# Own weight buffers for the projections, frames normed ahead, and an earlier place for tile 1 and the short tile

## The chip, the cores and the metric

The kernel runs on one core of a Trainium2 chip. The metric is the device time of one execution in microseconds (us). The engines named below are PE (matrix multiply), DVE (vector), ACT (scalar), POOL (which issues the indirect DMAs) and SP (which issues the other DMAs). Each engine takes its instructions in the order in which the program has them.

## The reference

One layer of a streaming encoder, for 1024 new frames (8 tiles of 128 frames, called 0 to 7) and for 32 frames of a running stream (the short tile, called S):

```python
h = rms_norm(x, norm_mix_w)
proj = h @ w_in                                   # 1024 -> 3608 columns
o1 = gla(...)                                     # gated linear attention, a recurrence over chunks
o2 = gated_delta_net(conv(...))                   # gated delta rule, a recurrence over chunks
x = x + concat(o1, o2) @ w_out
# PEER: 8 heads, product keys; 16 experts of 16384 for each head and frame
q = rms_norm(x, norm_ffn_w) @ peer_wq
eidx, gate = top_16_of_product_keys(q, k1, k2)    # 128 experts for each frame
act = gelu(einsum('thkd,td->thk', peer_u[eidx], xblk))
x = x + einsum('thk,thkd->td', gate * act, peer_v[eidx])
y = rms_norm(x, norm_final_w)
```

## The kernel before

The work falls into three parts that overlap in time.

**The mixers and the routing.** The input projections are made in four groups, PROJ = [0, S], [1, 2, 3], [4, 5, 6], [7], by the generator `project(g)`. It loads its tiles of x, norms and transposes them (three frames of 128 in a group of three, "its frames"; PE writes `ptr`), and then multiplies with chunks of `w_in` of 256 KB that `chunk` loads: 17 units by channel (PE writes `pcm`) and 6 by token (PE writes `ptm`). Groups 1 and 2 split weights and frames into a rounded part and a rest (`wh`, `wl`, `hh`, `hl`); groups 0 and 3 multiply float32 directly. For each tile, in the order 0, S, 1, 2, ... 7, come then the mixers: `gdn_free`, `gla`, and `gdn_state` (the part of the delta rule that needs the state of the tile before). When a group of tiles is through, `out_proj` (PE writes `pwo`) and `route` (PE writes `pq` and `psc`) follow, and `select`, a chain of small DVE operations that picks the 128 experts of each frame. At the end of `select` the row numbers `ef`/`ei` of the experts are made, and `prepare_rows` transposes them on PE (`pe`). Tile 0 is its own routing group; its rows come in two halves.

**The dense tiles.** For tiles 2 to 5 all 16384 experts are computed with matmuls (`dense`: PE writes `pD` and `pV`, in three passes each). Before that, `gate_matrix` lays their gates out.

**The gathered tiles.** For tiles 0, S, 1, 6 and 7 the rows of `peer_u` and `peer_v` are fetched with indirect DMAs that POOL issues, each of 128 rows of 1024 floats (512 KB). `u_phase(t)` fetches 128 such tiles `ug` (32 for S) and DVE multiplies each with the frames and sums it into a column of `act` (line 1063); after the last one, `act` goes through a gelu and PE transposes it (`pw`). `v_phase(t)` fetches 128 tiles `vg` (32 for S) in rounds of four, and PE adds each round up in eight matmuls (`pv`, line 1108). A u-tile of tile 0 or S uses the three buffers of the pool `ge`; in later tiles every fourth one uses a buffer of the pool `gp`, which is opened once the projections' pool `p1` is closed. `act` has two buffers.

What stands where on an engine is decided by a scheduler when the program is built. It starts from the order in which the generators are woven together (`weave` takes one step of each in turn); steps under `urgent` have a high priority. GATHERS gives the order of the gathered tiles.

## Time and profile before

| | |
|---|---|
| time, median of 3 runs | 3464.75 us (3453.7 to 3467.83) |
| the profiled execution | 3470.48 us, of which its span 3468.8 us |
| busy in the span | PE 90%, DVE 66%, POOL 38%, ACT 37% |
| DMA | 974.88 MB, mean 281 GB/s |
| chain that ended last | PE 66%, DVE 14%, DMA 10%, issue 5% |

The span can be cut at places that the trace shows: the last matmul of the first projection at 117 us, the first gather at 249 us, the last gather for tile 0 at 601 us, the first dense matmul at 1737 us, the last dense matmul at 3342 us. A busy PE is not a PE at its peak, since its matmuls are pipelined; float32 matmuls have two records each in the trace, the rounded ones (`pD`, `pV`, and the `pcm` and `ptm` of groups 1 and 2) have one.

### The profile page before, as it was taken

How to read it: one execution, taken by the hardware profiler on the slowest of the kernel's cores; microseconds unless marked ns; L12 is line 12 of the kernel's file. 1: busy time of each engine (PE TensorE's matmuls, PEld its weight loads, DVE VectorE, ACT ScalarE, POOL GpSimd, SP SyncE). 2: the span in 40 equal slices, each digit the busy share in tenths (PEclk: the TensorE clock that was granted, in tenths of full speed). 3: DMA queues.
4: the chain of work that ended last, by engine and by line, in shares of the span. 5: the costliest groups of instructions: out<-in, count | busy, mean ns of one | idle time of the engine just before them, and what ended most of it. 6: DMA issues, size and time to landing. Idle time of an engine off the chain costs nothing.

```text
span 3468.8 us, 50260 instructions
## 1 busy us (share of the span) xinstructions
PE 3113.4 (90%) x17730; PEld 2469.2 (71%) x17730; DVE 2305.9 (66%) x6165; ACT 1298.7 (37%) x2703; POOL 1312.4 (38%) x1168
## 2 busy tenths in 40 slices
PE   8873778999999888989589999999999999999974
PEld 6662677998898767877367777777777777777630
DVE  3557878664388998999867677766766765434420
ACT  5322445665323226899523232222222322212210
POOL 3004443000001354353545555555555553233454
PEclk9986878999999899989699999999999999999986
DMA  6368888445745789999999998989998997767898
GB/s 197 88 210 261 277 282 272 129 133 153 234 129 175 250 321 350 330 343 329 319 345 357 338 345 335 349 334 349 356 335 325 366 345 283 253 240 278 288 341 297
DMA packets 373455, 974.88 MB, mean 281 GB/s; under 512 B 37345, under 2 KB 139186, under 8 KB 369106
## 3 DMA queue, kind: packets, MB, share of 16 engines
q0 software_dynamic: 156672, 570.49, 45.8%
q1 hardware_dynamic: 216386, 400.64, 34.1%
q8 instruction: 140, 2.29, 0.3%
q14 instruction: 113, 0.93, 0.1%
q10 hardware_dynamic: 144, 0.52, 0.0%
HBM read 908.73 MB, written 62.76 MB: 280 GB/s over the span
## 4 chain that ended last, share of the span: by engine, by line
PE 66%; DVE 14%; DMA 10%; issue 5%; ACT 4%; POOL 1%; another core or an unknown queue 0%; SPq 0%; POOLq 0%; ACTq 0%; DVEq 0%
PE pV L186 6%; PE pD L187 6%; PE pV L188 6%; PE pV L187 6%; PE pD L186 6%; PE pD L188 6%; PE pv L1108 6%; PE pq L537 3%; DVE ug L1063 3%; PE pwo L501 3%; DMA ug<-u,ei 3%; DMA vg<-v,eiT 2%; PE ptm L440 2%; PE ptm L430 2%; PE pcm L332 1%
## 5 line engine op out<-in xcount | busy, mean ns | idle before, releaser
L1062 POOL DMA_INDIRECT ug<-u,ei x512 | 624.9, 1221 | 1111.5 <-DVE ug L1063 467.4
L1102 POOL DMA_INDIRECT vg<-v,eiT x488 | 567.5, 1163 | 895.9 <-PE pv L1108 450.3
L1063 DVE SCALAR_TENSOR_TENSOR ug<-ug,h 128x1024 f32<-128x1024 f32 x544 | 658.7, 1218 | 129.8 <-DMA ug<-u,ei 118.7
L187 PE MATMUL pD<-hh,ul 128*128 128x512 f32 x1024 | 402.2, 393 | 10.9 <-DVE ul L181 10.9
L186 PE MATMUL pD<-hh,uh 128*128 128x512 f32 x1024 | 402.0, 393 | 1.6 <-ACT uh L180 1.6
L188 PE MATMUL pD<-hl,uh 128*128 128x512 f32 x1024 | 401.8, 392 | 0.0
L187 PE MATMUL pV<-vh,wl 128*128 128x512 f32 x1024 | 398.7, 391 | 0.0
L188 PE MATMUL pV<-vl,wh 128*128 128x512 f32 x1024 | 398.2, 391 | 0.0
L186 PE MATMUL pV<-vh,wh 128*128 128x512 f32 x1024 | 378.4, 393 | 0.0
L1108 PE MATMUL pv<-vg,wd 128*32 128x512 f32 x1952 | 293.4, 661 | 57.7 <-DMA vg<-v,eiT 57.7
L180 ACT CAST vh<-vx 128x1024 fp32r<-128x1024 f32 x128 | 129.2, 1050 | 556.1 <-PE pV L187 471.7
L1003 DVE TENSOR_TENSOR acc<-acc,pV 128x512 f32<-128x512 f32 x256 | 168.8, 684 | 246.2 <-PE pV L188 228.0
L537 PE MATMUL pq<-h2T,wqb 128*128 128x256 f32 (+2 forms) x1280 | 257.8, 356 | 9.3 <-DMA wqb<-wq 6.4
L977 ACT ACTIVATE w<-pD 128x512 f32<-128x512 f32 x128 | 76.6, 598 | 504.3 <-PE pD L188 476.8
L537 PEld LDWEIGHTS pq<-h2T,wqb 128*128 128x128 f32 x1280 | 216.5, 198 | 35.1 <-DMA wqb<-wq 6.6
L187 PEld LDWEIGHTS pD<-hh,ul 128*128 128x128 f32 x1024 | 192.7, 188 | 66.0 <-issue 12.6
L186 PEld LDWEIGHTS pV<-vh,wh 128*128 128x128 f32 x1024 | 191.8, 188 | 58.8 <-issue 12.6
L186 PEld LDWEIGHTS pD<-hh,uh 128*128 128x128 f32 x1024 | 192.7, 188 | 54.5 <-issue 10.1
L188 PEld LDWEIGHTS pD<-hl,uh 128*128 128x128 f32 x1024 | 192.7, 188 | 52.5 <-issue 12.6
L188 PEld LDWEIGHTS pV<-vl,wh 128*128 128x128 f32 x1024 | 192.2, 188 | 51.0 <-issue 10.9
L187 PEld LDWEIGHTS pV<-vh,wl 128*128 128x128 f32 x1024 | 192.2, 188 | 47.1 <-issue 7.5
L180 ACT CAST wh<-w 128x512 fp32r<-128x512 f32 x244 | 149.9, 617 | 143.9 <-DVE w L983 53.3
(333 smaller groups left out, 5606.6 us busy)
## 6 DMA issues: line engine op xcount, KB each, us to landing
vx<-v SPq DMA_DIRECT2D x128, 512.0 KB
ux<-ut SPq DMA_DIRECT2D x127, 512.0 KB
wqb<-wq SPq DMA_DIRECT2D x80, 576.0 KB
gd<-gst SPq DMA_DIRECT2D x16, 2048.0 KB
G<-gd SPq DMA_DIRECT2D x32, 1024.0 KB
w<-win_c SPq DMA_DIRECT2D x96, 256.0 KB
wch<-wout SPq DMA_DIRECT2D x40, 512.0 KB
w<-win_t SPq DMA_DIRECT2D x72, 256.0 KB
```

The costliest lines, as they stand in the source:

```text
L180: nc.scalar.copy(hi, x)
L186: mm(out, a[0], b[0], start=first, stop=False, **kw)
L187: mm(out, a[1], b[0], start=False, stop=False, **kw)
L188: mm(out, a[0], b[1], start=False, stop=last, **kw)
L501: mm(p[:n, :P], mixT[t][:, kb, :], w[:, kb, :], start=(kb == 0), stop=(kb == KB - 1))
L537: mm(p[:, :N], w[:, kb, :], h2T[:, kb, :], start=(kb == 0), stop=(kb == KB - 1))
L977: nc.scalar.activation(w, pD, AF.Gelu_apprx_tanh)
L1003: nc.vector.tensor_tensor(acc[ti][:, cs], acc[ti][:, cs], p, op=ALU.add)
L1062: nc.gpsimd.indirect_dma_start(out=g, out_offset=None, in_=A["u"], in_offset=idx_of(ei[:, k:k + 1]))
L1063: nc.vector.scalar_tensor_tensor(g, g, 1.0, h2, op0=ALU.mult, op1=ALU.mult, accum_out=act[:, k:k + 1])
L1102: nc.gpsimd.indirect_dma_start(out=g, out_offset=None, in_=A["v"], in_offset=idx_of(eiT[:, tok:tok + 1]))
L1108: return mm(pv[half][c * 32:(c + 1) * 32, :], wd[:, c, :], vs[c][:, half * 512:(half + 1) * 512], start=(r == 0), stop=(r == ns - 1), tile ...
```

## The change

`project` takes its weight chunks from buffers of its own (`w`, two of them, in the pool `p1`), and no longer from the four `wqb` buffers that it shared with the routing; `wqb` has three. Group 0 turns through four kinds of buffers. Group 3, which had turned through `wqb`, `wh` and `wl`, eight buffers in all, has the two. The transposed frames of group 0 lie in the buffer `h2T`, and no longer in `hh`, which is group 1's from the start.

The frames of a group are normed and transposed ahead of its weights: `frames_of(1)` stands before tile 0, `frames_of(2)` behind tile S, `frames_of(3)` behind tile 2. Group 2 is woven with tile 2, group 3 with tile 3 (before: group 2 with tiles 1 and 2, group 3 with tile 2).

Tile 1 is treated as tile 0 was: its `gdn_state` follows at once, then the routing of the group [1, S] and the selection of both. The gathers begin with `peer_u` of 0, S and 1, all of them urgent, and `peer_v` of 0 follows.

```diff
-COMING = {1: [(1, None)], 2: [(2, 24)], 3: [(2, None), (3, None)]}
-
-BGN = [0, 0, 0, 0, 24, 14, 14, 14, 14, 14]
+COMING = {1: [1], 3: [2], 4: [3]}
+
+AT_ONCE = [0, 1]
+
+BGN = [0, 0, 0, 0, 14, 14, 14, 14, 14, 14]
...
+WQ = 3
...
-GATHERS = [([0, "S"], []), ([1], [0]), ([6], ["S", 1]), ([7], [6]), ([], [7])]
+GATHERS = [([0, "S", 1], []), ([], [0]), ([6], ["S", 1]), ([7], [6]), ([], [7])]
...
         if direct:
-            hx = p1.tile([P, KB, N], F32, name="hx", tag="hh")
+            hx = rt.tile([P, KB, N], F32, name="hx", tag="h2T") if first else p1.tile([P, KB, N], F32, name="hx", tag="hh")
...
             loads[0] += 1
-            own = direct and (None, "wh", None, "wl")[loads[0] % 4]
-            if own:
-                w = p1.tile(list(src.shape), F32, name="w" + own, tag=own, bufs=WB)
+            own = ("w", "wqb", "wh", "wl")[loads[0] % 4] if first else "w"
+            if own == "wqb":
+                w = rt.tile(list(src.shape), F32, name="w", tag="wqb", bufs=WQ)
             else:
-                w = rt.tile(list(src.shape), F32, name="w", tag="wqb", bufs=4)
+                w = p1.tile(list(src.shape), F32, name="w", tag=own, bufs=WB)
...
-            w = rt.tile([P, KB, P], F32, name="wch", tag="wqb", bufs=4)
+            w = rt.tile([P, KB, P], F32, name="wch", tag="wqb", bufs=WQ)
...
-            w = rt.tile([P, KB + 1, P], F32, name="wqb", tag="wqb", bufs=4)
+            w = rt.tile([P, KB + 1, P], F32, name="wqb", tag="wqb", bufs=WQ)
...
-            e = t in (0, "S") or k % 4 < 3
+            e = t in EARLY or k % 4 < 3
...
+    def frames_of(g):
+
+        weave(some(projects[g], len(PROJ[g])))
+
+    frames_of(1)
+    last = None
     for k in range(len(ORDER) + 1):
-        cur, prev = (ORDER[k] if k < len(ORDER) else None), (ORDER[k - 1] if k > 1 else None)
-        parts = [selecting(), some(behind, BGN[k])]
-        parts.append(chain(*(some(projects[g], n) for g, n in COMING.get(k, []))))
-        if prev is not None:
-            parts.append(gdn_state(prev))
+        cur = ORDER[k] if k < len(ORDER) else None
+        parts = [selecting(), some(behind, BGN[k]), chain(*(projects[g] for g in COMING.get(k, [])))]
+        if last is not None:
+            parts.append(gdn_state(last))
         if cur is not None:
             parts += inputs(cur)
         weave(*parts)
-        if k == 0:
-
+        if k in COMING and COMING[k][-1] + 1 in projects:
+            frames_of(COMING[k][-1] + 1)
+        ready_now = finished(last) if last is not None else []
+        last = cur
+        if cur in AT_ONCE:
             weave(gdn_state(cur))
-            finished(cur)
-            weave(routing(GROUPS[0]))
-            weave(selecting())
+            last = None
+            for g in finished(cur):
+                weave(routing(g))
+                weave(selecting())
...
-        us = [urgent(u_phase(t, *sel[t])) if t in (0, "S") else u_phase(t, *sel[t]) for t in us]
+        us = [urgent(u_phase(t, *sel[t])) if t in EARLY else u_phase(t, *sel[t]) for t in us]
```

What the scheduler makes of it shows in the order of the instructions, here at three places. The first is PE at the end of the routing of tile 0: `pq` and `psc` are the routing's matmuls, `pe` the transpose of the chosen row numbers `ef`, `ptr` a transpose of frames, `pcm` a unit of the projection of group 1. Before:

```order
L537 MATMUL pq<-h2T,wqb 128x128 x8
L543 MATMUL psc<-wqb,qb 128x128
L1035 MATMUL pe<-ident,ef 128x128
L313 MATMUL ptr<-ident,x 128x128 x24
L332 MATMUL pcm<-hh,wh 128x384 x4
L332 MATMUL pcm<-hl,wh 128x384 x4
```

And in the changed kernel:

```order
L540 MATMUL pq<-h2T,wqb 128x128 x8
L546 MATMUL psc<-wqb,qb 128x128
L1038 MATMUL pe<-ident,ef 128x128
L217 MATMUL psm<-ident,row 128x64 x3
L237 MATMUL pdg<-aA_132,tri 128x12
L374 MATMUL pn<-ones,sq 128x1 x3
L335 MATMUL pcm<-hh,wh 128x384 x4
```

The 24 transposes of frames are gone from here, and so are 264 of the 408 `pcm` matmuls of group 1: they stand ahead of these rows, among the mixers and the routing of tile 0. `pe` still stands right behind the last `psc`.

The second place is POOL's queue from the first gather on: `ug<-u,ei` is a gather of `peer_u` for tile 0 in the first row and for tile 1 in the later rows, `ug<-u,eiS` one for S, `vg<-v,eiT` one of `peer_v` for tile 0. Before:

```order
L1062 DMA ug<-u,ei 128x1024 x128
L1102 DMA vg<-v,eiT 128x1024 x5
L1062 DMA ug<-u,ei 128x1024
L1062 DMA ug<-u,eiS 128x1024 x32
L1062 DMA ug<-u,ei 128x1024 x6
L1102 DMA vg<-v,eiT 128x1024 x4
L1062 DMA ug<-u,ei 128x1024 x4
```

And in the changed kernel:

```order
L1065 DMA ug<-u,ei 128x1024 x128
L1065 DMA ug<-u,eiS 128x1024 x32
L1065 DMA ug<-u,ei 128x1024 x10
L1105 DMA vg<-v,eiT 128x1024 x4
L1105 DMA ug<-v,eiT 128x1024
L1105 DMA vg<-v,eiT 128x1024
L1065 DMA ug<-u,ei 128x1024 x118
```

Before, the gathers of `peer_u` for tile 1 and of `peer_v` for tile 0 take turns by fours; now 118 gathers for tile 1 stand in one piece, and nearly all of `peer_v` of tile 0 stands behind them.

The third place is the end of PE's program, at the last dense matmul (`pV`); `pv_28316` and `pv_28317` are the two halves of the sums of `peer_v` for tile 7. Before:

```order
L187 MATMUL pV<-vh,wl 128x512
L188 MATMUL pV<-vl,wh 128x512
L1108 MATMUL pv_28316<-vg,wd 32x512
L1108 MATMUL pv_28316<-ug,wd 32x512 x2
L1108 MATMUL pv_28316<-vg,wd 32x512
L1108 MATMUL pv_28317<-ug,wd 32x512 x2
```

And in the changed kernel:

```order
L190 MATMUL pV<-vh,wl 128x512
L191 MATMUL pV<-vl,wh 128x512
L1111 MATMUL pv_28316<-vg,wd 32x512 x4
L1111 MATMUL pv_28317<-vg,wd 32x512 x4
L1111 MATMUL pv_28316<-ug,wd 32x512 x4
L1111 MATMUL pv_28317<-ug,wd 32x512 x4
```

From the last `pV` to the end of the program there stand 152 `pv` matmuls before, which are 19 rounds of four gathers, and 56 in the changed kernel, which are 7 rounds.

## Rows read from the trace of the kernel before

**Rows 1.** The page: busy time by engine, and the chain that ended last.
```profile
PE 3113.4 (90%) x17730; PEld 2469.2 (71%) x17730; DVE 2305.9 (66%) x6165; ACT 1298.7 (37%) x2703; POOL 1312.4 (38%) x1168
PE 66%; DVE 14%; DMA 10%; issue 5%; ACT 4%; POOL 1%; another core or an unknown queue 0%; SPq 0%; POOLq 0%; ACTq 0%; DVEq 0%
```

**Rows 2.** Stretches: us, busy and (records) of PE, PEld, DVE, ACT, POOL; clock, DMA.
```profile
117.00:249.00 132.00, 110.85 (x913) 94.16 (x911) 78.42 (x397) 34.90 (x120) 0.00 (x0) 0.92 0.40 124
249.00:304.00 55.00, 5.24 (x39) 4.65 (x39) 43.03 (x154) 9.66 (x31) 23.74 (x25) 0.59 0.79 249
304.00:602.00 298.00, 222.64 (x1303) 205.36 (x1303) 237.07 (x521) 139.36 (x264) 124.69 (x104) 0.82 0.85 279
602.00:1093.00 491.00, 478.11 (x3534) 444.85 (x3534) 318.15 (x1277) 240.50 (x557) 5.63 (x6) 0.97 0.52 159
1093.00:1737.00 644.00, 541.55 (x3495) 448.93 (x3493) 593.32 (x2226) 382.37 (x1021) 282.05 (x232) 0.89 0.91 312
1737.00:3342.00 1605.00, 1591.79 (x7619) 1186.12 (x7619) 993.94 (x1449) 426.55 (x562) 778.07 (x655) 1.00 0.88 324
3342.00:3462.00 120.00, 62.28 (x306) 12.20 (x304) 7.84 (x20) 1.65 (x4) 65.66 (x69) 0.67 0.91 327
```

**Rows 3.** Waits in 304 to 601 us: us in total, times, longest.
```profile
PE pe L1035 <- DVE ef L1026: 48.9, 1, 48.9
DVE ug L1063 <- DMA ug<-u,ei: 37.3, 28, 3.4
```

**Rows 4.** Timeline of POOL: tile 0's first, fourth, one slow and last gather.
```profile
249.28 1.13 POOL L1062 DMA_INDIRECT ug<-u,ei  x1 [211.23 <-DVE vt L552]
...
255.32 1.34 POOL L1062 DMA_INDIRECT ug<-u,ei  x1 [2.42 <-DVE vt L549]
...
366.26 3.86 POOL L1062 DMA_INDIRECT ug<-u,ei  x1 [0.30 <-issue]
...
600.59 0.94 POOL L1062 DMA_INDIRECT ug<-u,ei  x1 [2.00 <-DVE ug L1063]
```

**Rows 5.** Groups on DVE and POOL, 249 to 602 us, and POOL after 3342.
```profile
L1063 DVE SCALAR_TENSOR_TENSOR ug<-ug,h 128x1024 f32<-128x1024 f32 x125 | 152.3, 1220 | 49.9 <-DMA ug<-u,ei 48.7 <-issue 0.6 <-DVE XT L741 0.2
L1062 POOL DMA_INDIRECT ug<-u,ei x128 | 148.4, 1160 | 415.1 <-DVE vt L552 213.2 <-DVE ug L1063 129.8 <-DVE hist L392 9.7
L1102 POOL DMA_INDIRECT vg<-v,eiT x37 | 35.2, 953 | 24.8 <-PE pv L1108 16.2 <-issue 8.5
```

**Rows 6.** Timeline of POOL: the first, fourth and last gather for S.
```profile
1111.07 0.94 POOL L1062 DMA_INDIRECT ug<-u,eiS  x1 [24.04 <-DMA eiS<-ei]
...
1118.10 0.94 POOL L1062 DMA_INDIRECT ug<-u,eiS  x1 [3.61 <-DVE ug L1063]
...
1197.29 0.94 POOL L1062 DMA_INDIRECT ug<-u,eiS  x1 [0.99 <-DVE sc L551]
```

**Rows 7.** Timeline of PE: a round in the dense stage and its neighbours.
```profile
3303.36 0.39 PE L187 MATMUL pD<-hh,ul 128*128 128x512 f32 x1
3303.59 0.39 PE L188 MATMUL pD<-hl,uh 128*128 128x512 f32 x1
3303.91 1.92 PE L1108 MATMUL pv<-vg,wd 128*32 128x512 f32 x16
3305.76 0.50 PE L186 MATMUL pD<-hh,uh 128*128 128x512 f32 x1
```

**Rows 8.** Timeline of PE: tile 7's first round, the last pV, rounds behind it.
```profile
3253.94 1.06 PE L1108 MATMUL pv<-vg,wd 128*32 128x512 f32 x8
...
3341.92 0.39 PE L188 MATMUL pV<-vl,wh 128*128 128x512 f32 x1
3343.12 0.62 PE L1108 MATMUL pv<-vg,wd 128*32 128x512 f32 x1 [0.81 <-DMA vg<-v,eiT]
...
3362.34 3.40 PE L1108 MATMUL pv<-vg,wd 128*32 128x512 f32 x16 [3.35 <-DMA vg<-v,eiT]
3367.83 2.76 PE L1108 MATMUL pv<-ug,wd 128*32 128x512 f32 x16 [2.09 <-DMA ug<-v,eiT]
...
3457.96 1.03 PE L1108 MATMUL pv<-vg,wd 128*32 128x512 f32 x1 [6.61 <-DMA vg<-v,eiT]
```

**Rows 9.** The chain in order of time: start us, us, what.
```profile
57.58 4.13 DMA wwl<-win_t
...
370.42 7.24 DMA ug<-u,ei
...
574.85 5.60 DMA w<-win_s
...
600.95 1.90 PE ptr L313 x8
...
606.61 5.88 PE pcm L332 x32
...
1154.10 8.42 DMA ug<-u,eiS
```

**Rows 10.** Waits of PE in 1093 to 1737 us.
```profile
PE pq L537 <- DMA wqb<-wq: 6.4, 1, 6.4
```

**Rows 11.** A group on ACT, 250 to 602 us.
```profile
L95 ACT ACT_TABLE_LOAD x10 | 12.8, 1283 | 0.2
```

More of the change, by code (lines that the diff above doesn't have):

```diff
@@ L275, in project @@
             if t == tiles[0]:
-                nmix = rt.tile([P, D], F32, name="nmix", tag="wqb", bufs=4)
+                nmix = rt.tile([P, D], F32, name="nmix", tag="wqb", bufs=WQ)
                 nc.sync.dma_start(nmix, bass.AP(tensor=A["nmix"].tensor, offset=A["nmix"].offset, ap=[[0, P], [1, D]]))
@@ L516, in route @@
         h2T = rt.tile([P, KB, N], F32, name="h2T", bufs=1)
-        nffn = rt.tile([P, D], F32, name="nffn", tag="wqb", bufs=4)
+        nffn = rt.tile([P, D], F32, name="nffn", tag="wqb", bufs=WQ)
         nc.sync.dma_start(nffn, bass.AP(tensor=A["nffn"].tensor, offset=A["nffn"].offset, ap=[[0, P], [1, D]]))
@@ L1229, in layer_kernel @@
             gp = ctx.enter_context(tc.tile_pool(name="gp", bufs=1, side="right", reuse_waits="tile"))
-        for g in finished(prev) if prev is not None else []:
+        for g in ready_now:
             behind = chain(behind, routing(g))
```

## The prediction

> **What bounds the kernel now.** The page first: PE is busy in 90% of the span and holds 66% of the chain that ended last, DVE 14%, DMA 10% [rows 1]. Such shares mix stages, so the stretches come next [rows 2], and they show five regimes. From 117 to 249 us PE works on tile 0's mixers and routing, with 21 of 132 us idle. From 249 to 304 us it does next to nothing (5.2 us): the waits name it, 48.9 us of PE standing at `pe` for the row numbers `ef` [rows 3]. From there to 602 us, while `peer_u` of tile 0 is gathered, PE is idle for a quarter, and DVE is busy for 237 of 298 us. From 602 to 1093 us POOL is all but idle (5.6 us) and PE is the bound (478 of 491 us). From 1093 to 1737 us DVE is (593 of 644). The dense stage is PE's alone (1592 of 1605, clock 1.00). Behind the last `pV` comes a tail of 120 us in which PE waits for gathers, at a clock of 0.67.
>
> **The change, step by step.** The sum is made against the profiled execution: 3470.5 us, its span and 1.7 us around it, 5.7 us over the median of the runs.
>
> *The tail.* 19 rounds follow the last `pV`, now 7. The first starts at 3343.12 and the nineteenth at 3457.96 [rows 8]: 18 steps, 6.4 us each. 12 rounds fewer: -77 us.
>
> *The dense stage.* The order puts 102 rounds between the first `pD` and the last `pV`, where 92 were. A round stretches the step between two dense matmuls from 0.23 us to 2.17 us [rows 7], so it costs PE 1.9 to 2.0 us: +20 us. Can the gathers keep up? The order spaces tile 7's 25 rounds there by 31 to 32 matmuls, 24 dense ones and one round, some 7.4 us. Before, 13 rounds of tile 7 went from 3253.94 to the one just ahead of the last `pV` [rows 8], 7 us apart, with PE busy throughout. I take no wait.
>
> *Tile 0 up to its first gather (249.28 us, [rows 4]).* 24 transposes and 264 `pcm` matmuls now lie ahead of it on PE. 32 `pcm` take 5.88 us, 8 transposes 1.90 [rows 9]: 264 x 0.184 + 24 x 0.24 = 54 us. 21 fit into PE's idle time, if that can be used at all: +33 (bounds 0 and +54). The 48.9 us at `pe` stay, because nothing was put between the last `psc` and it; the filling work went ahead of the wait and lengthens the way to it.
>
> *`peer_u` of tile 0.* 127 steps from 249.28 to 600.59 [rows 4], 2.77 us each, over three buffers; the order puts 540 DVE instructions beside them, where 529 were, so I keep the 352 us. What is gained is that PE stands at its 2,354th matmul at the end, and not at its 1,880th.
>
> *From there to PE's 4,147th matmul*, where the projections are about done in the changed kernel; before it stood there at 1093 us. PE's rate in 602 to 1093 us is 2,267 matmuls in 491 us. Now 1,793 are left: 388 us. Two things are new in this stretch. The selections of tiles 1 and S end in a `pe` again: up to the first of them there are 445 matmuls, 97 us, but 499 DVE instructions, at 0.25 us (318 us for 1,277 records) 125 us: +28 (bounds 0 and +49, a wait like tile 0's). And S's 32 gathers stand packed, with 228 matmuls (49 us) beside them. Before, S took 86 us for 31 steps; its first buffer came round in 7.0 us [rows 6], which over three buffers is 2.3 us a gather. 32 of these and one landing come to about 87: +38 (bounds 0 and +50). Sum 388 + 28 + 38 = 454 against 491, which with the 33 from above leaves PE 4 us ahead.
>
> *From the 4,147th matmul to the dense stage.* Tile 1's gathers can't go on before: `act` has two buffers, tile 1 takes tile 0's, and the transpose `pw` that frees it stands there, because its PSUM bank is the projections' until then. The DVE work up to the dense stage is the same (1,644 instructions, 1,653 before). But 118 gathers of tile 1 now stand in one piece, on three buffers, 5 to 6 DVE instructions apart (tile 0's: 4). That is near tile 0's case: 2.77 us a gather, 327 us, with DVE busy 79% (280 of 353 us; 48.7 us go at the landings of `ug` [rows 2, 5]) instead of the 92% of 1093 to 1737 us. 327 x (1 - 0.79/0.92) = +46 (bounds 0, if the landings are covered as they were, and +99, at 3.2 us a gather).
>
> Edits taken as nothing: `wqb` with three buffers for four (`pq` waited 6.4 us for it in 644 [rows 10]; twice that would be +6); 22 more table loads on ACT at 1.28 us [rows 11], 28 us, hidden on an engine that is busy for 382 of 644 us, and 28 if each came where others wait; group 0's nine buffers for eight; the frames normed ahead.
>
> Sum: +33 - 37 + 46 = +42 for the start of the dense stage, +20 in it, -77 behind it: -15. On the profiled execution that is 3455, on the median 3450 us.
>
> **A rule weighed.** POOL needs 1160 ns to issue a gather while DVE is 79% busy and 953 ns when DVE is nearly idle [rows 2, 5]; one took 3.86 us, and the next waited for nothing but that [rows 4]. The Trainium skill ("SBUF — State Buffer", section "SBUF: two separate sides") says that the descriptors of POOL's DMAs are written through a port that certain DVE operations hold for their whole length, so that such a DMA looks blocked by DVE. By that rule the piece of 118 gathers beside a busy DVE would be the wrong place for them; its example, some 3,100 ns in place of 620, would make 118 x (3.1 - 2.77) = +39 us. The trace shows 0.2 us of it, which POOL's 415 us of idle time in that stretch swallow.
>
> **The rivals.** *Tile 1 starves DVE* (the slower side). A buffer comes round in a landing and a product: 7.24 + 1.22 us over three buffers is tile 0's pace, 8.42 + 1.22, a landing of S's, makes 3.2 us a gather [rows 5, 9]: 118 x 0.45 = +53 on the forecast, 3503 us. For it: the routing's weights and the gate matrices run beside it. Against it: the DMA engines' share was 0.84 to 0.85 in tile 0's stretch too, and the pace there was 2.77. It decides from 3.05 us a gather on (33 us over the forecast).
>
> *The waits are hidden.* If S's packed gathers, the selection and tile 1's piece cost no more than their DVE work, 28 + 38 + 46 = 112 us fall away: 3338 us; with half of it, which is more likely, 3394. For it: in 304 to 601 us DVE waited for only 28 landings, 3.4 us at most [rows 3]. Against it: tile 0's pace, with the same buffers.
>
> *Group 3 lacks buffers.* It had eight weight buffers and has two, for 58 chunks, with 630 matmuls of PE's order about them, 137 us, 2.4 us a chunk. A chunk takes 4.1 to 5.6 us to land [rows 9] and about 0.9 in use; over two buffers that is 2.5 to 3.3 us: +6 to +52, up to 3502. SP takes its DMAs in order, so a chunk that waits for its buffer holds up the routing's weights behind it.
>
> *The tail only moves.* If the 12 rounds that went into the dense stage wait there as they did behind it (2 to 3.8 us of PE's idle time each [rows 8]), +36: 3486 us. The 13 of before speak against it.
>
> *POOL is held up by DVE*, as the 3.86 us of [rows 4] was: 118 x 1.09 = +129, 3579 us. It was the exception among 128.
>
> **How the numbers follow.** The sum as it stands, give or take 20 us, has 45 in 100; the hidden waits 22, tile 1 starved 17, group 3 eight, the tail five, POOL three. A measurement of this kernel tells about 0.5% (17 us) from no change. So below 3447 us there are the second case and nearly half of the first: 0.42. Above 3482 lie tile 1, group 3, POOL and a part of the tail's case: 0.29, and 0.29 in between. The range reaches to the half-hidden case and past the starved one, 3385 to 3515 us; the first case alone has 3430 to 3470.
>
> **What would show it.** Behind the last `pV` some 45 us with 7 rounds; a dense stage of 1625 us that starts at about 1780 us; tile 0's first gather at 280 us and a wait of PE at `pe` of about 50 us right behind it; tile 1's 118 gathers in one piece of 310 to 340 us. I would be wrong if the dense stage starts before 1740 us (the waits were hidden) or after 1815 (tile 1 or group 3), or if PE shows idle time at `pv` before the last `pV`.

## The result, and the profile after

The changed kernel takes 3510.7 us (median of 4 runs, 3504.6 to 3513.2), the kernel before beside it 3466.3 us: a ratio of 1.0129, with a 95% interval of 1.0096 to 1.0162. The forecast was 3450 us; the time lies inside the range, on its slower side.

The page first: busy time by engine and the chain that ended last, as [rows 1].

```profile
PE 3130.6 (89%) x17730; PEld 2497.2 (71%) x17730; DVE 2316.9 (66%) x6165; ACT 1327.2 (38%) x2725; POOL 1282.3 (37%) x1168
...
PE 61%; DVE 13%; DMA 11%; issue 11%; ACT 3%; POOL 1%; SPq 0%; POOLq 0%; another core or an unknown queue 0%; ACTq 0%; DVEq 0%
```

PE has the same 17,730 records and 17 us more busy time, in a span that is 38 us longer (3507.1, before 3468.8). A page like this can't say where they went. The stretches of the changed kernel can (columns as in [rows 2]); their bounds are the legs of the prediction: the first gather, the end of `peer_u` of tile 0, PE's 4,147th matmul, its 5,000th, the first `pD`, the last `pV`. A matmul's number is its place in the program's order, looked up in the trace; two kernels with different orders can have different matmuls under one number.

```profile
117.00:301.00 184.00, 168.77 (x1251) 149.37 (x1251) 116.35 (x509) 78.68 (x191) 0.00 (x0) 0.95 0.46 142
301.00:353.00 52.00, 9.29 (x59) 8.01 (x57) 37.65 (x151) 12.24 (x36) 24.52 (x21) 0.60 0.75 238
353.00:679.00 326.00, 257.39 (x1628) 236.95 (x1629) 245.39 (x534) 127.70 (x259) 129.65 (x107) 0.85 0.82 273
679.00:906.00 227.00, 181.25 (x1127) 163.50 (x1127) 195.70 (x846) 96.39 (x238) 35.24 (x34) 0.83 0.48 156
906.00:1148.00 242.00, 225.36 (x1735) 210.88 (x1734) 122.59 (x404) 131.39 (x267) 3.17 (x3) 0.97 0.58 175
1148.00:1496.00 348.00, 275.60 (x1640) 245.07 (x1639) 324.81 (x1111) 139.79 (x388) 129.73 (x120) 0.85 0.84 277
1496.00:1839.00 343.00, 278.97 (x1871) 215.86 (x1869) 266.28 (x1083) 246.21 (x630) 133.13 (x123) 0.90 0.93 321
1839.00:3453.00 1614.00, 1612.03 (x7778) 1189.54 (x7778) 965.58 (x1398) 424.72 (x557) 772.55 (x663) 1.00 0.88 325
3453.00:3507.00 54.00, 20.48 (x114) 4.20 (x112) 5.81 (x9) 3.29 (x8) 21.25 (x22) 0.74 0.75 271
```

The dense stage is PE's alone as before (1612 of 1614 us), and 54 us follow the last `pV` where 127 did. What is lost lies ahead: the dense stage starts at 1839 us and not at 1737. The row to remember is 1148 to 1496 us: DVE is busy for 93% of it and PE for 79%. Three more views fill this in. First the timeline of POOL (start, length, what ended the idle time): tile 0's first and last gather, S's first, the first of tile 1, the first behind the wait for `act`, the first and the last of the 118 in one piece.

```profile
301.21 1.13 POOL L1065 DMA_INDIRECT ug<-u,ei  x1 [261.26 <-DVE ei L1030]
...
678.58 1.08 POOL L1065 DMA_INDIRECT ug<-u,ei  x1 [2.35 <-DVE ug L1066]
...
827.64 0.94 POOL L1065 DMA_INDIRECT ug<-u,eiS  x1 [147.98 <-DVE row L403]
...
905.73 1.15 POOL L1065 DMA_INDIRECT ug<-u,ei  x1 [1.75 <-DVE ug L1066]
...
1150.14 1.68 POOL L1065 DMA_INDIRECT ug<-u,ei  x1 [237.89 <-DVE ug L1066]
...
1175.75 0.94 POOL L1065 DMA_INDIRECT ug<-u,ei  x1 [0.30 <-DVE it L556]
...
1533.76 1.15 POOL L1065 DMA_INDIRECT ug<-u,ei  x1 [1.53 <-DVE ug L1066]
```

Then the waits from 301 to 679 us, which answer to [rows 3]:

```profile
PE pe L1038 <- DVE ef L1029: 39.6, 1, 39.6
...
DVE ug L1066 <- DMA ug<-u,ei: 56.2, 45, 3.5
```

And the timeline of PE at the last `pV`, which answers to [rows 8]:

```profile
3452.96 0.39 PE L191 MATMUL pV<-vl,wh 128*128 128x512 f32 x1
3453.35 1.92 PE L1111 MATMUL pv<-vg,wd 128*32 128x512 f32 x16
3461.41 3.64 PE L1111 MATMUL pv<-ug,wd 128*32 128x512 f32 x16 [6.14 <-DMA ug<-v,eiT]
3468.54 3.62 PE L1111 MATMUL pv<-vg,wd 128*32 128x512 f32 x16 [3.49 <-DMA vg<-v,eiT]
```

The 114 records behind 3453 us are seven rounds of 16 and two of the last `pV`. The first round stands ready at 3453.35; the next two come 8.1 and 7.1 us later, near the pace of before (6.4).

Against the forecast, leg by leg (us, profiled executions, before and after):

| leg | before | after | change | forecast |
|---|---|---|---|---|
| to tile 0's first gather | 249 | 301 | +52 | +33 |
| `peer_u` of tile 0, 127 steps | 351 | 377 | +26 | 0 |
| from there to PE's 4,147th matmul | 495 | 469 | -25 | -37 |
| from there to the dense stage | 642 | 691 | +49 | +46 |
| dense stage | 1605 | 1614 | +9 | +20 |
| behind the last `pV`, to the span's end | 127 | 54 | -73 | -77 |

### The profile page after: what moved, and what is told of

It is laid out like the page before. It is cut to its first block, busy times and chain, and to the rows that moved or that the text cites. A ratio compares the mean times of both kernels' runs of the same rounds, so it can differ in the third digit from the quotient of the medians.

```text
span 3507.1 us, 50218 instructions
## 1 busy us (share of the span) xinstructions
PE 3130.6 (89%) x17730; PEld 2497.2 (71%) x17730; DVE 2316.9 (66%) x6165; ACT 1327.2 (38%) x2725; POOL 1282.3 (37%) x1168
## 4 chain that ended last, share of the span: by engine, by line
PE 61%; DVE 13%; DMA 11%; issue 11%; ACT 3%; POOL 1%; SPq 0%; POOLq 0%; another core or an unknown queue 0%; ACTq 0%; DVEq 0%
PE pV L189 7%; PE pD L190 7%; PE pV L190 7%; PE pD L191 7%; PE pD L189 7%; PE pV L191 7%; PE pv L1111 6%; DMA ug<-u,ei 5%; DVE ug L1066 4%; PE pq L540 3%; PE pcm L335 2%; PE pgm L941 1%; PE ptm L433 1%; POOL ug L1065 1%; PE pga L630 1%
## 5 line engine op out<-in xcount | busy, mean ns | idle before, releaser
L1065 POOL DMA_INDIRECT ug<-u,ei x512 | 605.8, 1183 | 1325.5 <-DVE ug L1066 734.4
L1105 POOL DMA_INDIRECT vg<-v,eiT x432 | 487.6, 1129 | 537.8 <-PE pv L1111 396.7
L1111 PE MATMUL pv<-vg,wd 128*32 128x512 f32 x1728 | 258.8, 615 | 20.9 <-DMA vg<-v,eiT 20.9
```

The source lines that it names most:

```text
L1065: nc.gpsimd.indirect_dma_start(out=g, out_offset=None, in_=A["u"], in_offset=idx_of(ei[:, k:k + 1]))
L1105: nc.gpsimd.indirect_dma_start(out=g, out_offset=None, in_=A["v"], in_offset=idx_of(eiT[:, tok:tok + 1]))
L1111: return mm(pv[half][c * 32:(c + 1) * 32, :], wd[:, c, :], vs[c][:, half * 512:(half + 1) * 512], start=(r == 0), stop=(r == ns - 1), tile ...
```

## The experiments

The change has three parts, and I named a theory after each. **A**: the work put ahead of tile 0's first gather (part 1: the projections' own weight buffers and frames ahead) is lost. **B**: routing tiles 1 and S at once, with a second wait at `pe` and S's gathers packed (part 2), is what costs. **C**: tile 1's gathers in one piece ahead of tile 0's rounds (part 3). A fourth, **D**, was that POOL's idle time from 906 to 1148 us is missed later. The new weaving of the projections (COMING) goes with part 2 here: every kernel below has it but the kernel before, e5 and e7. The table has the legs of fifteen kernels beside the two compared (us, profiled executions), and the ratio of the times to the kernel before with its 95% interval.

| kernel | first gather | 127 steps | 4,147th matmul at | to the 5,000th | dense at | dense | behind | ratio |
|---|---|---|---|---|---|---|---|---|
| before | 249 | 351 | 1095 | 294 | 1737 | 1605 | 127 | 1 |
| changed | 301 | 377 | 1148 | 349 | 1839 | 1614 | 54 | 1.0129 (1.0096-1.0162) |
| e1, parts 2, 3 | 263 | 341 | 1201 | 352 | 1876 | 1626 | 10 | 1.0109 (1.0082-1.0135) |
| e2, parts 1, 3 | 299 | 371 | 1091 | 354 | 1816 | 1622 | 96 | 1.0191 (1.0169-1.0213) |
| e3, parts 1, 2 | 300 | 374 | 1143 | 270 | 1788 | 1623 | 27 | 0.9922 (0.9898-0.9946) |
| e5, part 1 | 301 | 365 | 1088 | 289 | 1747 | 1601 | 143 | 1.0075 (1.0055-1.0094) |
| e6, part 2 | 262 | 343 | 1210 | 260 | 1841 | 1641 | 8 | 1.0002 (0.9981-1.0022) |
| e7, part 3 | 264 | 353 | 1111 | 353 | 1845 | 1624 | 81 | 1.0222 (1.0203-1.0241) |
| e4, changed, 3 `act` | 300 | 370 | 1199 | 274 | 1845 | 1613 | 8 | 0.9994 (0.9978-1.0011) |
| e10, e3 with 3 `act` | 307 | 375 | 1212 | 273 | 1860 | 1646 | 8 | 1.0113 (1.0093-1.0133) |
| e8, changed, 4 buffers | 307 | 384 | 1164 | 381 | 1888 | 1638 | 8 | 1.0108 (1.0089-1.0127) |
| e9, quarter products | 300 | 373 | 1148 | 275 | 1774 | 1628 | 62 | 0.9995 (0.9981-1.0009) |
| e14, tile 0's rounds woven in | 303 | 372 | 1146 | 256 | 1769 | 1626 | 38 | 0.9935 (0.9914-0.9955) |
| e13, changed, no frames | 266 | 353 | 1207 | 356 | 1915 | 1631 | 28 | 1.0291 (1.0255-1.0328) |
| e12, e3, no frames | 264 | 355 | 1209 | 259 | 1831 | 1622 | 30 | 1.0008 (0.9993-1.0023) |
| e15, changed, group 3 | 302 | 370 | 1164 | 361 | 1867 | 1622 | 8 | 1.0132 (1.0097-1.0167) |
| e11, e3, group 3 | 300 | 373 | 1160 | 246 | 1771 | 1630 | 8 | 0.9839 (0.9819-0.9859) |

### One part undone, and one part alone

Undone in e1, the core of part 1:

```diff
-WQ = 3
+WQ = 4
...
-            own = ("w", "wqb", "wh", "wl")[loads[0] % 4] if first else "w"
+            own = direct and (None, "wh", None, "wl")[loads[0] % 4]
...
-    frames_of(1)
```

In e2, part 2:

```diff
-AT_ONCE = [0, 1]
+AT_ONCE = [0]
```

In e3, part 3:

```diff
-GATHERS = [([0, "S", 1], []), ([], [0]), ([6], ["S", 1]), ([7], [6]), ([], [7])]
+GATHERS = [([0, "S"], []), ([1], [0]), ([6], ["S", 1]), ([7], [6]), ([], [7])]
...
-            e = t in EARLY or k % 4 < 3
+            e = t in (0, "S") or k % 4 < 3
```

(In e3 tile 1 isn't urgent either, and in e1 `hx` is back under its old tag and the later frames aren't normed ahead. e2 keeps the new weaving of the projections.)

> The changed kernel with the weight buffers, the place of hx and the frames of the projections put back as before (four shared wqb buffers, no frames ahead); tiles 0, S, 1 first and routing at once stay. Nothing of the computation is left out. In its order 136 pcm matmuls stand ahead of tile 0's first gather, not 400, and 1 round behind the last pV, not 7; 103 in the dense stage, 32 ahead of it. Theory A, that the work put ahead of tile 0's first gather is what makes the dense stage start 102 us late (it came in front of the wait at pe and used none of the idle time it was to fill): first gather back at about 250 us, 352 us for peer_u of tile 0, dense stage from about 1765 (1839 less 51 and 26), then 1615, then some 10 us: about 3395 us. Theory B, that the loss is in the packed selections and gathers of S and 1 further on: the first gather comes at 250 too, but PE's work only moves behind it, the dense stage starts at 1820 or later, and only the tail is gained: about 3450.

> The changed kernel with only tile 0 routed at once, as before; tile 1 and S are routed behind the next tiles. Nothing of the computation is left out. Its order has 20 rounds ahead of the dense stage, 102 in it and 14 behind the last pV. Theory B, that the selections of tiles 1 and S ahead of a wait at pe and S's packed gathers (679 to 906 us, 46 us of PE idle there) are the loss: the dense stage starts 40 to 50 us earlier, at about 1795, the tail takes 90: about 3500 us. Theory A (the front) or C (tile 1's packed gathers): it starts at 1830 or later, and with the longer tail the time is 3535 or more.

> The changed kernel with the old order of the gathers: tile 0 and S first, tile 1's gathers behind them as a filler and on four buffers, not first and on three. Nothing of the computation is left out. Its order has 30 rounds ahead of the dense stage, 103 in it and 3 behind the last pV. Theory C, that tile 1's packed gathers with DVE 95% busy from 1237 to 1535 us are the late loss (691 us from PE's 4,147th matmul to the dense stage, 642 before): dense stage from about 1790, then 1617, then 20: about 3430 us. Theories A and B: dense stage from 1839 as in the changed kernel, 3478 us.

Theory C's numbers came: 3440 us for e3, with the dense stage at 1788 (expected 3430 and 1790). Theory A falls in its plain form: in e1 the first gather is back at 263 us and its 127 steps at 341, but PE's 4,147th matmul comes at 1201, 53 us later than in the changed kernel, and the time is 3510 us, not the 3395 or 3450 written down. B falls too: e2 starts its dense stage 23 us earlier, but has 96 us behind the last `pV`, and is the slower one. Then each part alone, made by the same edits on the kernel before (in e5 only group 1's frames go ahead):

> The kernel before with the first part of the change alone (weight buffers of their own, three wqb, the frames of group 1 ahead). Nothing of the computation is left out. If the three parts add up, the three kernels with one part undone give P1 0.0%, P2 -0.8%, P3 +1.9% (P1 + P2 = -0.8, P2 + P3 = +1.1, P1 + P3 = +1.9), and this one takes 3470 us. Its first gather comes at about 300 us, with a loss of 50 us there that is made up later, since PE has those projections behind it. Its order has 22 rounds behind the last pV where before has 19, so if the loss in front is not made up it takes 3540.

> The kernel before with the second part alone (tiles 1 and S routed at once, the projections in the new order); weight buffers, frames and the order of the gathers as before. Nothing of the computation is left out. No round stands behind the last pV, 34 ahead of the dense stage, 102 in it. If the parts add up: 3443 us. If P1 in front costs its 52 + 26 us and is not made up, this one is the best, with the dense stage from about 1730 and a time of 3365 us.

> The kernel before with the third part alone (tile 1's peer_u in front of everything, on three buffers and urgent). Nothing of the computation is left out. 22 rounds ahead of the dense stage, 102 in it, 12 behind the last pV where before has 19. If the parts add up: 3537 us, since tile 1's products then fill DVE from 1100 to 1500 us and the dense stage starts 100 us later than before, at 1835. If P3 costs only beside P2's packed S: 3430 (the tail is 45 us shorter).

Part 3 costs wherever it is put in: +2.2% alone, +1.2% on part 1 (1.0075 to 1.0191; from e5 to e2 the weaving of the projections changes besides), +1.1% on part 2 (1.0002 to 1.0109), +2.1% on both (0.9922 to 1.0129). Parts 1 and 2 don't add up as expected. Alone they cost 0.75% and nothing; together they gain 0.8%. e6 shows why: routing at once, with the new weaving, puts the projections off (4,147th matmul at 1210 us, before 1095), and part 1, which has frames and weights at hand, takes 67 us of this back (e3, 1143).

The column to read is the one up to the 5,000th matmul. Every kernel with part 3 and `act`, place and products as changed has 349 to 381 us there, every other one 246 to 294. Here is that leg, 853 matmuls by number, in e3 (columns as in [rows 2]):

```profile
1143.00:1414.00 271.00, 249.55 (x1648) 204.97 (x1647) 240.62 (x979) 85.43 (x267) 144.00 (x121) 0.96 0.91 328
```

Beside 1148 to 1496 us of the changed kernel: the same number of PE's records (1648 and 1640), 271 us and 348, PE idle for 21 us and for 72, and a granted clock of 0.96 and 0.85. DVE does 84 us more work in the changed kernel. The groups of DVE in the two legs say what it is (columns as in [rows 5]). In the changed kernel:

```profile
L1066 DVE SCALAR_TENSOR_TENSOR ug<-ug,h 128x1024 f32<-128x1024 f32 x114 | 138.1, 1215 | 19.7 <-DMA ug<-u,ei 18.5 <-issue 1.2
L1066 DVE DVE_READ_ACCUMULATOR ug<-ug,h 128x1 f32 x114 | 9.3, 82 | 0.0
```

And in e3:

```profile
L1066 DVE SCALAR_TENSOR_TENSOR ug<-ug,h 128x1024 f32<-128x1024 f32 x66 | 79.5, 1212 | 5.3 <-DMA ug<-u,ei 2.9 <-issue 2.4
```

48 products more, at 1.22 us and 0.08 for the reading of the sum: 62 of the 84 us. DVE waited for landings for 18.5 us in all.

The 853 matmuls are not the same ones, though. e3 has 13 rounds of tile 0 in this leg (208 records of `pv`); the changed kernel has none, and 200 records more of `pgm`, the gate matrices of the dense tiles. For these DVE makes `gA` and `gB`, 36 of each and 11 in e3, 34 us more (other work is some 12 us less), and ACT scales `gA`. PE's longest wait in the changed kernel's leg stands there; in e3 it is 1.0 us:

```profile
L933 DVE TENSOR_TENSOR gB<-iota,gmf 128x512 f32<-128x512 f32 x36 | 24.8, 689 | 2.1 <-PE pgm L941 2.1
L935 DVE TENSOR_TENSOR gA<-iota,gmf 128x512 f32<-128x512 f32 x36 | 24.6, 685 | 0.0
...
PE pgm L941 <- ACT gA L938: 29.8, 14, 7.6
```

Are the gate matrices what costs, and not the products? e5 has nearly as many of them in its leg of 289 us (1088 to 1377), and few products:

```profile
L1064 DVE SCALAR_TENSOR_TENSOR ug<-ug,h 128x1024 f32<-128x1024 f32 x63 | 76.1, 1212 | 8.9 <-DMA ug<-u,eiS 8.0 <-DMA h<-h2d 1.0
L933 DVE TENSOR_TENSOR gA<-iota,gmf 128x512 f32<-128x512 f32 x30 | 20.2, 675 | 0.0
...
PE pgm L939 <- ACT gA L936: 3.3, 5, 1.5
```

So 30 pairs without the packed products cost little. Over all kernels the leg goes with the products in it: 18 to 71 of them where it takes 246 to 294 us, 109 to 128 where it takes 349 to 381 (e9, below, has 98 short ones).

### Landings or DVE's own time

The prediction had the piece slowed by landings (**L**); the rows above speak for DVE's time (**V**). Four edits bear on it: a fourth buffer, products of a quarter of the columns (three quarters of tile 1's dot products left out), tile 0's rounds woven in again, a third `act`.

In e8:

```diff
-            e = t in EARLY or k % 4 < 3
+            e = t in (0, "S") or k % 4 < 3
```

In e9:

```diff
+            m = D // 4 if t == 1 else D
-            nc.vector.scalar_tensor_tensor(g, g, 1.0, h2, op0=ALU.mult, op1=ALU.mult,
+            nc.vector.scalar_tensor_tensor(g[:, :m], g[:, :m], 1.0, h2[:, :m], op0=ALU.mult, op1=ALU.mult,
```

In e14:

```diff
-GATHERS = [([0, "S", 1], []), ([], [0]), ([6], ["S", 1]), ([7], [6]), ([], [7])]
+GATHERS = [([0, "S"], []), ([1], [0]), ([6], ["S", 1]), ([7], [6]), ([], [7])]
```

> The changed kernel with tile 1's gathers still first and urgent, but on four buffers (three of ug and one of the right side, as they had before), not three. Nothing of the computation is left out. Theory L (the prediction's): tile 1's piece is paced by landings, so a fourth buffer takes the pace from 2.5 to 2.0 us a gather and the dense stage starts 40 us earlier, at 1800 us. Theory V: DVE is the limit there (busy 282 of 298 us), the packed products keep the other DVE work from PE, and a fourth buffer only packs them closer: the dense stage starts at 1839 or later. 32 rounds ahead of the dense stage and none behind the last pV in its order, so the time is 3425 by L and 3465 to 3480 by V.

> The changed kernel, with tile 1's products over a quarter of the columns: the gathers, their buffers and their place stay as they are, but three quarters of each of tile 1's dot products are left out (the computation is changed in that). A product of 1.2 us on DVE should then take about 0.4. Theory V (DVE's time beside tile 1's gathers is what PE lacks from its 4,147th to its 5,000th matmul, 348 us, where the kernels without the third part take 260 to 294): about 100 us of DVE work less, that stretch at 260 us, the dense stage from about 1755; 9 rounds behind the last pV: 3430 us. Theory L (landings, the gathers' DMA traffic or POOL's issue set the pace): the stretch stays within 20 us of 348, and the time within 20 us of 3520.

> The changed kernel with tile 1's gathers behind tile 0 and S and woven with tile 0's rounds, as before, but still urgent and still on three buffers. Nothing of the computation is left out. 32 rounds ahead of the dense stage, 99 in it, 5 behind the last pV; in its order tile 1's gathers reach as far as the dense stage again. If it is their place alone that costs, PE's 4,147th to 5,000th matmul takes about 270 us, as with the third part undone, and the time is 3440 to 3460. If urgency and the three buffers cost too, that stretch stays above 310 and the time above 3480.

In e8 the fourth buffer does speed the gathers. The last 117 of tile 1 start 2.68 us apart on average, though three of `peer_v` stand among them; in the changed kernel it is 3.08 (1177.00 to 1533.76):

```profile
1195.71 0.93 POOL L1065 DMA_INDIRECT ug<-u,ei  x1 [0.30 <-DMA vg<-v,eiT]
...
1506.94 1.15 POOL L1065 DMA_INDIRECT ug<-u,ei  x1 [15.49 <-DVE ug L1066]
```

But PE has nothing from it: with 128 products in the leg and not 114 it takes 381 us, the dense stage starts at 1888 us, and the time is 3512 us (theory V had 1839 or later, and 3465 to 3480). (Its profiled execution took 3535 us, 23 over its median; less 23 the leg would still be 358.) e9 shortens the products and leaves the pace. Its leg:

```profile
1148.00:1423.00 275.00, 253.25 (x1648) 229.08 (x1647) 228.01 (x1153) 110.84 (x337) 101.93 (x104) 0.96 0.91 314
```

And the products in it:

```profile
L1067 DVE SCALAR_TENSOR_TENSOR ug<-ug,h 128x256 f32<-128x256 f32 x98 | 40.9, 418 | 43.4 <-DMA ug<-u,ei 43.4
```

A product takes 0.42 us and not 1.22. Tile 1's last 118 gathers still take 362 us (1166.42 to 1528.82; in the changed kernel 358), and DVE waits *more* for landings, 43.4 us. But PE's leg falls from 349 to 275 us and the dense stage comes 65 us earlier. The leg alone is not a clean comparison, since the scheduler's order shifts in e9 too, from 1157 us on (22 pairs of `gA` and `gB` lie in the leg, where 36 did; rounds of tile 0 there are none in either). The start of the dense stage is a cleaner one: all products of tiles 0, S and 1 and all gate matrices stand ahead of it in both kernels, and e9 has three rounds fewer there, some 6 us of PE at 2 us each. The gathers' pace and the landings are not what PE pays for; DVE's time is. The time of 3467 us is over the 3430 expected: the dense stage starts 19 us later than written down (15 of them in that leg) and takes 1628 us, 14 more than in the changed kernel.

e14 keeps urgency and three buffers and changes the place alone: 256 us, 3444 us, near e3's 3440. So the place is the whole of part 3's cost. Its leg (55 products):

```profile
1146.00:1402.00 256.00, 244.10 (x1648) 201.16 (x1647) 230.00 (x962) 82.34 (x256) 141.56 (x116) 0.97 0.93 341
```

The third `act`, on the changed kernel (e4) and on e3 (e10):

```diff
-        act = gs.tile([P, P], F32, name="act", bufs=2)
+        act = gs.tile([P, P], F32, name="act", bufs=3)
```

> The changed kernel with three buffers for act where it has two, so that tile 1's peer_u need not wait for the transpose of tile 0 at PE's 4,147th matmul (906 to 1160 us, POOL busy for 7.8 us of 254). Nothing of the computation is left out. Its order has 42 rounds ahead of the dense stage, 94 in it and none behind the last pV. Theory D, that the idle POOL of 906 to 1160 us is what the late leg lacks: tile 1's gathers run from 906 to about 1300 us, the dense stage starts at about 1800, takes 1600 and has no tail: 3405 us. Theory A: the dense stage is set by PE's and DVE's work up to there and starts at 1839 or later (15 more rounds stand ahead of it, 2 us of PE each, +30): 1869 + 1600 = 3470 us.

> The changed kernel with the old order of the gathers and, besides, three buffers for act. Nothing of the computation is left out. Its order has 35 rounds ahead of the dense stage, 101 in it and none behind the last pV. If the third buffer for act is worth what it was in the changed kernel (3511 to 3469 us there, of which about half was the tail), this one takes 3420 us; if it only helped by taking tile 1's products out of the packed stretch, which the old order does too, the tail's 20 us are gained and the earlier gathers cost PE its 15 us back: 3435.

With a third `act` tile 1's gathers go on at 906 us, and the leg behind drops to 274 us; but the leg ahead, in which PE had been the bound, grows. Here it is in e4, with the place of the 4,147th matmul as its end:

```profile
906.00:1199.00 293.00, 249.29 (x1725) 230.58 (x1724) 223.06 (x589) 118.54 (x259) 101.22 (x95) 0.88 0.83 273
```

The changed kernel ran as many matmuls in 242 us with DVE at 122.59 busy. The products cost where they are put, 51 us here, with DVE busy for 76% of the leg. The dense stage starts at 1845, and D's 1800 is off; e4's 3468.5 us is what theory A forecast (3470), but what it gained is the tail, 54 us to 8. In e10, where tile 1's products had been spread well, the third buffer only harms: 3512 us, against 3420 to 3435 expected; 69 us of it up to the 4,147th matmul, and 23 more in the dense stage, which I can't account for.

### The front

On the changed kernel (e13) and on e3 (e12):

```diff
-    frames_of(1)
```

> The changed kernel with the old order of the gathers and without the frames of group 1 normed ahead of the loop; the weight buffers stay. Nothing of the computation is left out. 136 pcm, not 400, stand ahead of tile 0's first gather; 30 rounds ahead of the dense stage, 102 in it, 4 behind the last pV. If work in front of tile 0's first gather is lost (the wait at pe is not filled by it), the first gather comes at 262 us and not at 300, and the dense stage 30 us earlier, at 1758: 3410 us. If it only moves (the kernel with the second part alone had its gather at 262 and its dense stage at 1841), 3440 to 3480.

> The changed kernel without the frames of group 1 normed ahead of the loop; all else as changed. Nothing of the computation is left out. 136 pcm, not 400, stand ahead of tile 0's first gather; 30 rounds ahead of the dense stage, 103 in it, 3 behind the last pV. The prediction gave the work in front +33 us up to the first gather and nothing behind it, and counted the earlier projections as a gain; measured were +52 and +26. If that is the price of this work and PE is paid back by it, the first gather comes at 264 us, its 127 steps take 355 us, and PE's 4,147th matmul still comes 50 us or more later than in the changed kernel (1148 us), at about 1205; dense stage at 1880, time 3520. If the work in front is a plain loss, PE's 4,147th matmul comes at 1090, the dense stage at 1780, time 3415.

e12 comes out as its second case had it, e13 as its first, and further: the dense stage at 1915 us for 1880, 3570 us for 3520. Without the frames the first gather comes 35 and 36 us earlier (e13 and e12) and its 127 steps take 24 and 19 us less, and at the 4,147th matmul these kernels are 59 and 66 us *behind*: 3570 and 3475 us. (They have a low clock on the way to the first gather, 0.50 from 139 to 165 us, which the kernel before and the changed one have not; see the last section.) The work in front has the price that the legs show, and is paid back with as much again.

### Group 3, and two repeats

On the changed kernel (e15) and on e3 (e11):

```diff
-            own = ("w", "wqb", "wh", "wl")[loads[0] % 4] if first else "w"
+            own = ("w", "wqb", "wh", "wl")[loads[0] % 4] if direct else "w"
```

> The changed kernel with the old order of the gathers and with four kinds of weight buffers for groups 2 and 3 too, not w alone (the rival that group 3 lacks buffers). Nothing of the computation is left out. Its order has 34 rounds ahead of the dense stage, 102 in it and none behind the last pV. If group 3 lacks buffers, the projections up to PE's 4,147th matmul get 6 to 52 us shorter (904 to 1148 us in the changed kernel) and the time is 3430 or less; if not, that stretch stays at 240 to 245 us, and the time is 3425 to 3445, by the tail alone.

> The changed kernel with four kinds of weight buffers for groups 2 and 3 too, not w alone. Nothing of the computation is left out. 33 rounds ahead of the dense stage, 103 in it, none behind the last pV. If group 3 lacked buffers in the changed kernel (a rival of the prediction), the stretch from PE's 3,043rd to its 4,147th matmul (904 to 1148 us) gets 6 to 52 us shorter. If not, that stretch stays within 10 us of 244 (it was 12 us longer beside the old order of the gathers), and what is gained is the tail and what the order brings: 3455 to 3480 us.

PE's wait for weights in the changed kernel, 904 to 1148 us, was this:

```profile
PE pcm L331 <- DMA w<-win_c: 2.1, 3, 1.2
...
PE ptm L433 <- DMA w<-win_t: 0.3, 1, 0.3
```

2.4 us in all; with more buffers the stretch from the 3,043rd matmul got longer, 263 us in e15 and 256 in e11. For this stretch the rival falls. e15's time of 3506 us is over the 3455 to 3480 expected: the tail went, but its dense stage starts at 1867. Yet e11 is the fastest kernel here, 3414.3 us, a ratio of 0.9839: it starts its dense stage 17 us before e3 and has nothing behind the last `pV`. Why a longer stretch leads to a shorter leg behind it (246 us for 270) was not tried; in its row from 1160 to 1406 us PE is at 96% busy:

```profile
1160.00:1406.00 246.00, 236.75 (x1638) 195.70 (x1637) 232.54 (x954) 80.97 (x258) 140.70 (x115) 0.99 0.95 356
```

> The kernel before, unchanged, for another profile: its tile 0 had the first gather at 249 us with TensorE's granted clock at 1.00 from 139 to 165 us, while the four kernels with the same 136 pcm ahead of it (only the first part undone, the second or the third part alone, no frames) had it at 262 to 266 us and two of them a clock of 0.50 in that stretch. If the clock there differs from one execution to the next, the first gather comes at 262 to 266 us here, and the work put in front cost 36 us and not 52. If it comes at 249 again, the four kernels owe their 15 us to something else in their order.

> The changed kernel, unchanged, for another profile. All eleven profiles with the frames of group 1 ahead had tile 0's first gather at 299 to 307 us; this one too, with a clock of 0.9 or more from 139 to 165 us. PE's 4,147th matmul at 1145 to 1165 us, its 5,000th 345 to 380 us behind it, dense stage from 1835 to 1890 us.

Both repeats show their kernels' legs again: the kernel before has its first gather at 250 us, a clock of 1.00 from 139 to 165 us and the dense stage at 1723 (3453 us); the changed one 301, 1155 and 1841 us (3508 us). So the kernel before's early first gather is not one execution's chance, and e16's expectation of 262 to 266 falls; more on this at the end.

## Why the prediction was wrong, by its own steps

**The tail, the dense stage and the late leg** came near the sizes worked out: -73 for -77, +9 for +20, +49 for +46; the last of these by luck, as shown below. PE has no idle time at `pv` ahead of the last `pV` to speak of (1612 of 1614 us busy), so the rival *the tail only moves* falls.

**The step that failed** is the price of the work put in front, and with it what part 1 buys up to the 4,147th matmul: "+33" for tile 0 up to its first gather, "I keep the 352 us" for `peer_u` of tile 0, and "388 us" for the 1,793 matmuls that are left. Together (388 against 491) they made part 1 worth 33 + 0 - 103 = -70 us there, before the 28 and 38 us that the selection and S's gathers cost. e5, part 1 alone, measures -7: +52, +14 and, from the end of `peer_u`, 421 us for 495 (-74). In the changed kernel the first two terms miss by 19 and 26 us, 45 of the 57 us that the sum is off here. The three errors:

- Of PE's 21 idle us ahead of the first gather, 15 are still idle (184 - 168.77), so 6 were filled and not 21. The prediction had "if that can be used at all" and a bound of +54; the bound was the value.
- With the frames ahead, the 127 steps of tile 0 took 365 to 384 us in twelve profiles; without, 341 to 355 in seven. DVE's count of instructions, on which the 352 rested, was no measure: DVE is busy for 283 us where it was for 280, and idle for 95 where it was for 73. Landings are 7.5 us of this (56.2, and 48.7 in [rows 5]); the rest is spread over small waits, and why the work ahead brings them stays open.
- In e5 PE stands at its 2,292nd matmul when tile 0's gathers end, not at the 2,354th, and takes 227 ns for a matmul behind it, where 491 / 2,267 gave 217. That makes 33 us. (The changed kernel itself stands within some ten matmuls of the 2,354th.)

What part 2 costs there was near enough beside part 1: 28 + 38 = 66 forecast; from e2 to the changed kernel 57 us (1091 to 1148). (S's 38 was summed 3 to 4 us too high: 32 gathers at 2.34 us and a landing of 8.4 come to 83 us, not 87.) Taken in the other order the split is another: part 2 alone costs 115 us (e6, 1210 for 1095), and part 1 on top of it gives back 67. In the sum these steps gave -4 us and were +53. That, and not the late leg, turned a forecast of 15 us faster into a span 38 us longer.

**The late leg** had its size and not its cause. "DVE busy 79%", with the rest lost at landings, is wrong: it was busy for 93% up to the 5,000th matmul. The sign "after 1815 (tile 1 or group 3)" came, with the dense stage at 1839, but it pointed at the wrong leg: this one took 3 us more than forecast. Tile 1's 118 gathers took 3.06 us each (1175.75 to 1533.76), which is the rival *tile 1 starves DVE* by its number (from 3.05 us on) and not by its mechanism: DVE wasn't starved but full, with 114 products among the small operations and the gate matrices that PE waits for. e9 shows it by shortening the products, e8 by packing them closer. Behind them DVE is 78% busy (266 of 343 us), where e3 has 347 of 374: the work that was pulled forward is missing there, and 31 of the 78 us come back.

So the change lost because of part 3. Undoing it is worth 70 us of the profiled span: 78 in the leg behind the 4,147th matmul and 27 behind the last `pV`, less 31 given back ahead of the dense stage and 8 in it, and 4 by which e3 was ahead already. The prediction had that cost, and would have had to hold parts 1 and 2 against it one by one.

**The other rivals and the edits at nothing.** *The waits are hidden*: no, the dense stage starts at 1839, not before 1740. *Group 3 lacks buffers*: no, above. *POOL is held up by DVE*: POOL's 114 issues for tile 1 beside a DVE that is 93% busy took 1078 ns each, not more than the 1160 of [rows 5] (the idle time in this row has in it the 238 us ahead of its first gathers):

```profile
L1065 POOL DMA_INDIRECT ug<-u,ei x114 | 122.9, 1078 | 452.2 <-DVE ug L1066 308.9 <-DVE vt L555 29.9 <-DVE i L873 14.0
```

By the rule of the Trainium skill that the prediction weighed ("SBUF — State Buffer", section "SBUF: two separate sides"), these issues should have looked blocked if the products are among the DVE operations that it means; the trace shows no such block beside them. `wqb` with three buffers: PE waited for it once, 4.2 us. The 22 more table loads on ACT came (155 for 133); what they cost was not tried.

## What to carry to other kernels

When work that several engines share is moved earlier, ask which engine is full at the new place: 48 products of 1.2 us more, and 25 pairs of gate matrices with them, where DVE was 89% busy cost PE 78 us, though DVE waited for landings for only 18.5 us. Spread such filler over the stretch in which its engine has room, and look at the leg it leaves as well as at the one it enters. And price a change of several parts one part at a time: here the one gain, which needs two parts together, was hidden by a third.

## What the runs showed of the hardware

The granted clock can differ between two kernels on a stretch in which their instructions are the same ones in the same order. e7's order differs from that of the kernel before only far behind, on POOL from 907 us on and on PE from the 4,460th matmul. Yet from 139 to 165 us its clock is 0.50 (the lower level, 1.2 GHz), where the kernel before has 1.00, in both of its profiles. Here are e7's rows, 110 to 120 and 139 to 165 us (columns as in [rows 2]):

```profile
110.00:120.00 10.00, 8.45 (x43) 5.03 (x41) 3.03 (x9) 4.99 (x8) 0.00 (x0) 1.00 0.47 140
139.00:165.00 26.00, 25.22 (x114) 22.20 (x115) 8.18 (x33) 2.39 (x11) 0.00 (x0) 0.50 0.03 8
```

And those of the kernel before:

```profile
110.00:120.00 10.00, 9.66 (x47) 5.54 (x46) 1.52 (x4) 4.67 (x7) 0.00 (x0) 1.00 0.56 180
139.00:165.00 26.00, 23.08 (x190) 19.56 (x188) 14.46 (x59) 6.96 (x25) 0.00 (x0) 1.00 0.05 11
```

From 110 to 120 us PE was idle for 1.55 us in e7 and for 0.34 in the other; but e7 is some 2 us ahead there (its first projection ends at 114.9 us, not 116.6), so the rows do not cover quite the same instructions. From 139 to 165 us e7 falls from 2 to 13 us behind, and its first gather comes at 264 us for 249. The five other kernels without the frames ahead, e7 among them, have 0.50 to 0.56 in this stretch and the first gather at 262 to 266. Why the clock falls in them and not in the kernel before was not found. The Trainium skill ("TensorE: Matmul & The Clock Gate", "Part 1: The HAM clock gate (the "warmup" mystery)") says that the clock depends on how busy the engine has lately been and that this varies from run to run; here it went with the kernel, as far as two profiles of the one and one each of the five others can tell.
